# Seven block products for eight in four K-tile pairs of the down product

## The chip, the cores and the metric

The kernel is one program on one core of a Trainium2 chip. The time is the device time of one execution in microseconds (us); the result of a comparison is the ratio of the times of two kernels that run on the same chip. A core has a matrix engine (TensorE, PE in the profile), a vector engine (VectorE, DVE), an engine for functions and copies (ScalarE, ACT), a general one (GpSimd, POOL), and a queue engine that here only starts loads (SyncE, SP). Each engine executes its own list of instructions in order and waits for others by semaphores. SP, ACT and POOL also start DMAs, which run beside the engines.

## What is computed

The kernel is one layer of a diffusion backbone on 256 latent tokens of width 2048, with 256 context tokens ahead of them. A gated linear attention and a differential attention share one input projection, are merged by gates, projected, and added to x. Then comes a gated MLP with a depthwise convolution of width 3:

```
h2 = modulate(rms_norm(x_new, norm2_w), sh2, sc2)
u = h2 @ w_up                                   # 2048 -> 2 x 5632
u = sum(pad(u)[:, j:j + T] * conv_w[j] for j in range(3)) + conv_b
gate, val = split(u, 2)
x_new = x_new + g2 * ((silu(gate) * val) @ w_down)   # 5632 -> 2048
```

Only the last line matters here: a product of the 256 x 5632 matrix g = silu(gate) * val with w_down (5632 x 2048), then the multiplication by the row g2 and the addition of x_new. All is float32. So that PE can work at its fast rate, each operand is split into a high half (rounded to the fast format, fp32r) and a low half (the rest), and a product of two blocks is three matmuls: high by high, low by high, high by low.

## The kernel before

The down product goes over two halves h of the 2048 output columns, 1024 each. Within a half it goes over 44 K tiles k of 128 rows of w_down. For a K tile, fetch (L225) starts one load of 128 x 1024 on SP into one of 4 places called raw; pieces (L1292) cuts it into two pieces of 512 columns, and split (L201) makes of each its high half whi (a cast on ACT, L206) and its low half wlo (a subtraction on DVE, L213). The halves lie in 4 places each (tags hi and lo), so that a new piece can be cast when the piece four before it has been read for the last time. For each piece, part (L1297) does three matmuls for each of the two blocks t of 128 tokens: 12 matmuls of 512 columns per K tile. They accumulate in four banks of PSUM (2 blocks of tokens by 2 blocks of columns). `after(i, chain[0])` ties each matmul of the stage behind the one before it, so PE's order is that of the program. The first half's banks are the four aux banks, the second half's the four acc banks.

g comes as 44 tiles gs[k] of 128 x 2 x 256: index 1 holds the high half, index 0 the low half. The last one is finished while the down product begins.

The residual must be added in the layout of the result (tokens on partitions), but x_new lies transposed in the C tiles (tags c0 to c15). turn(m) (L1265) transposes four of them by 4 STREAM_TRANSPOSE on DVE into one place of araw and then copies 32 pieces from there into the row tiles by 32 small DMAs that POOL starts. It is done four times. gate_line(h) (L1253) makes the row g2 for one half: a memset on POOL of a place of araw, four small DMAs on POOL that gather the values in one partition, and three that spread it to others; a STREAM_SHUFFLE on DVE (L1284) then spreads it to all partitions, into cb, and frees the place. The tag araw has two places. They were used by the loads of w_ada (with their dot products on DVE, L338) until the end of the up stage; then by two lines and four turns. done (L1307) finishes a bank: times cb, plus the row tile, both on DVE, and a store that ACT starts. residual(h, k) (L1277) puts these steps into the program behind chosen K tiles.

The order in which an engine meets its instructions is that of a planner at build time (`schedule_with_timeline_sim=True`, L1344). It goes through the program with estimates of its own of how long each instruction takes. When an engine is free in that reckoning, the planner gives it the earliest instruction of the program that is ready by then, that is, whose operands are there and whose tile has a place. So a step written far down in the program can be hoisted far up; and a step may stand far down in an engine's list because the planner reckoned that its place or its operand would come late. The list is fixed then: the chip's engines take it in that order, however long the things before truly take.

Of the kernel before, what the change touches and what calls it, by code (L numbers as in the profile page):

```python
# [9 lines left out]
F32 = mybir.dt.float32  # L10
F32R = mybir.dt.float32r
# [3 lines left out]
ALU = mybir.AluOpType  # L15
# [3 lines left out]
P = 128  # L19
D = 2048  # L20
T = 256
# [7 lines left out]
FT = FF // P  # L29
# [9 lines left out]
SWW = 32 + C0 + (NGK + 1) * P  # L39
UPS = 6  # L40
CONVS = 7
SLOTS = 12
EARLY_ADA = 4, 14
GATE_ADA = [0.25] * 4 + [0.5] * 16 + [1] * 12
# [102 lines left out]
def layer_kernel(tc, I, out):  # L147
    nc = tc.nc
    V, S, G, PE = nc.vector, nc.scalar, nc.gpsimd, nc.tensor
    es = ExitStack()  # L150
    with es:
        cp = es.enter_context(tc.tile_pool(name="const", bufs=1))
        st = es.enter_context(tc.tile_pool(name="stream", bufs=1))
        hp = es.enter_context(tc.tile_pool(name="acts", bufs=1))
        ps = es.enter_context(tc.tile_pool(name="psum", bufs=1, space=PSUM))

        def acc_bank(name):
            return ps.tile([P, 512], F32, tag="acc", bufs=4, name=name)

        def aux_bank(name, j=0):  # L160
            return ps.tile([P, 512], F32, tag=f"aux{j}", bufs=2, name=name)
# [31 lines left out]
        chain = []  # L193
# [36 lines left out]
        def split_act(hi, lo, x):  # L230
            S.copy(hi, x)
            V.tensor_tensor(lo, x, hi.bitcast(F32), op=ALU.subtract)
# [965 lines left out]
        with tc.tile_pool(name="ffn", bufs=1) as pf:  # L1198
            gs = []
            ada_buffers(st, 2)  # L1200
            temps = [0]

            def temp():

                temps[0] += 1
                return C[temps[0] % (KT - UPS)][:, 1, :]


            def conv(b, ct):
                u = temp()  # L1210
                S.activation(u, b, AF.Identity, bias=vcol("conv_b", ct), scale=vcol("conv_w", 2 * FT + ct))
                V.scalar_tensor_tensor(u[:, 1:], b[:, :T - 1], vcol("conv_w", ct), u[:, 1:],
                                       op0=ALU.mult, op1=ALU.add)
                V.scalar_tensor_tensor(u[:, :T - 1], b[:, 1:], vcol("conv_w", 4 * FT + ct), u[:, :T - 1],
                                       op0=ALU.mult, op1=ALU.add)
                return u

            def gated(j, bg, bv):
                ug = conv(bg, j)
                uv = conv(bv, FT + j)  # L1220
                after(S.activation(ug, ug, AF.Silu), silu)
                V.tensor_tensor(ug, ug, uv, op=ALU.mult)
                g = pf.tile([P, 2, T], F32R, name=f"g{j}")
                split_act(g[:, 1, :], g[:, 0, :], ug)
                gs.append(g)

            def orders(n, nq, first, last):


                shifted = [i for j in range(0, nq * (last - first + 1) - 3, 7) for i in (first * nq + j, first * nq + j + 4)]  # L1230
                q = range(n * nq, (n + 1) * nq)
                return [ENDED if i == (last + 1) * nq - 1 else SHIFTED if i in shifted else TURN for i in q]

            for j in range(UPS // 2):
# [12 lines left out]
            ada_done(48)  # L1247

            splits[1] = 0
            gt = pf.tile([P, 32], F32, name="gt")  # L1250
            rows = []

            def gate_line(h):  # L1253

                line = st.tile([P, 1024], F32, tag="araw", bufs=2, name="line")
                G.memset(line, 0.0)
                to = line[0:1, :].rearrange("o (c p j) -> o c p j", c=8, p=4)
                for p in range(4):
                    o = 32 * p + 16 + 8 * h
                    nc.gpsimd.dma_start(to[:, :, p, :], gt[o:o + 8, :])  # L1260
                for r in range(32, P, 32):
                    nc.gpsimd.dma_start(line[r:r + 1, :], line[0:1, :])
                return line

            def turn(m):  # L1265

                rows.append([hp.tile([P, 512], F32, tag=f"a{4 * t + m}", name="row") for t in range(2)])
                turned = st.tile([P, 1024], F32, tag="araw", bufs=2, name="turned").rearrange("p (c t) -> p c t", c=4)
                for c in range(4):
                    V.transpose(turned[:, c, :], x1[4 * m + c])  # L1270
                for p in range(4):
                    for q in range(8):
                        to = rows[m][q // 4].rearrange("p (c n) -> p c n", c=4)
                        nc.gpsimd.dma_start(to[32 * (q % 4):32 * (q % 4 + 1), :, 32 * p:32 * (p + 1)],  # L1274
                                            turned[32 * p:32 * (p + 1), :, 32 * q:32 * (q + 1)])

            def residual(h, k):  # L1277

                if (h, k) == (0, 2):
                    V.transpose(gt, adav[:, 32:64])  # L1280
                elif (h, k) in ((0, 3), (0, 4)):
                    lines.append(gate_line(k - 3))
                elif (h, k) in ((0, 14), (0, 15)):
                    V.stream_shuffle(cb[:, 1024 * (k - 14):1024 * (k - 13)], lines[k - 14], [0] * 32)  # L1284
                elif (h, k) in ((0, 16), (0, 17), (1, 2), (1, 3)):
                    turn(len(rows))
                elif h and 8 <= k < 12:
                    done(0, k % 2, k // 2 % 2)

            lines = []  # L1290

            def pieces(k):  # L1292

                raw = fetch(I["w_down"][h, k], 1024)
                return [split(raw[:, n * 512:(n + 1) * 512], 512) for n in range(2)]

            def part(t, n, k, w):  # L1297
                ts = slice(t * P, (t + 1) * P)
                g = gs[k]
                for a, b in ((1, 0), (0, 0), (1, 1)):  # L1300
                    i = PE.matmul(banks[h][t][n], g[:, a, ts], w[n][b], start=k == 0 and (a, b) == (1, 0),  # L1301
                                  stop=k == FT - 1 and b == 1)
                    if chain:
                        after(i, chain[0])
                    chain[:] = [i]

            def done(h, t, n, cols=slice(0, 512)):  # L1307

                o = slice(1024 * h + 512 * n + cols.start, 1024 * h + 512 * n + cols.stop)
                y = hp.tile([P, 512], F32, tag=f"a{8 + (4 * h + 2 * t + n + (cols.start > 0)) % 8}", name="y")[:, :cols.stop - cols.start]  # L1310
                V.tensor_tensor(y, banks[h][t][n][:, cols], cb[:, o], op=ALU.mult)
                V.tensor_tensor(y, y, rows[2 * h + n][t][:, cols], op=ALU.add)
                nc.scalar.dma_start(out[t * P:(t + 1) * P, o], y)

            banks = []
            for h in range(2):
                banks.append([[acc_bank("down") if h else aux_bank("down", t) for n in range(2)] for t in range(2)])
                last = FT - 2 if h else FT
                for k in range(last):
                    w = pieces(k)  # L1320
                    for n in range(2):
                        for t in range(2):
                            part(t, n, k, w)
                    residual(h, k)

            ws = [pieces(k) for k in range(last, FT)]
            for n in range(2):
                for t in range(2):
                    for k in range(last, FT):
                        part(t, n, k, ws[k - last])  # L1330
                    for cols in [slice(0, 512)] if not (n and t) else [slice(0, 256), slice(256, 512)]:
                        done(1, t, n, cols)

# [14 lines left out]
```

## Time and profile before

| | us |
|---|---|
| median of 3 runs | 1696.35 (1695.54 to 1697.02) |
| the profiled execution | 1695.98 |
| its span, first to last instruction | 1693.8 |
| PE busy | 1674.0 (99%) |
| DVE busy | 1273.2 (75%) |
| ACT busy | 980.3 (58%) |
| POOL busy | 331.4 (20%) |
| down product, first to last matmul's start | 1449.4 to 1688.6 |

Times in rows are microseconds from the span's start. A row of a timeline gives the start, the length, the engine, the line of the kernel, the operation, the tiles written and read, and in brackets the idle time before it with what ended it. PEld is the loading of PE's stationary operand, which runs beside the matmuls. A matmul's length in the records is longer than the distance to the next, since matmuls overlap. "DMA to landing" is the time from a load's issue to its arrival.

### The profile page before, as it was taken

The page shows a single profiled execution, that of the slowest core. Times are in us where ns is not written, and L with a number is a line of the kernel's source. Part 1 is how long each engine was busy: PE and PEld are TensorE (multiplying, and loading weights), DVE is VectorE, ACT ScalarE, POOL GpSimd, SP SyncE. Part 2 cuts the span into 40 slices and gives each one's busy share as a digit, 9 for nine tenths or more (in the row PEclk, how much of TensorE's full clock was granted, in tenths as well). Part 3 has the DMA queues.
Part 4 walks back from the last instruction along what each step waited for, and adds up shares of the span by engine and source line. Part 5 has one row for each costly group of instructions (what it writes and reads, how often), then busy time and mean ns, then how long its engine had stood idle before and what let it go on. Part 6 is the DMA issues. An engine that isn't in the chain of part 4 may idle for free.

```text
span 1693.8 us, 28588 instructions
## 1 busy us (share of the span) xinstructions
PE 1674.0 (99%) x10108; PEld 1444.6 (85%) x10108; DVE 1273.2 (75%) x2426; ACT 980.3 (58%) x1984; POOL 331.4 (20%) x431
## 2 busy tenths in 40 slices
PE   7999999999999999999999999999999999999998
PEld 6779899998787888888888998888888888888887
DVE  5556766767688888788998797878888787755655
ACT  5324554756355777656665686666666666544443
POOL 0000213131210100001323200222222222684000
PEclk9999999999999999999999999999999999999999
DMA  9995533434567555687877556767777676676664
GB/s 384 402 408 194 169 120 98 137 113 145 191 199 234 169 187 185 205 284 268 269 263 264 185 195 218 231 229 234 236 237 238 225 238 221 201 225 203 219 193 143
DMA packets 110830, 370.82 MB, mean 219 GB/s; under 512 B 14432, under 2 KB 19552, under 8 KB 110688
## 3 DMA queue, kind: packets, MB, share of 16 engines
q1 hardware_dynamic: 102112, 362.51, 63.9%
q10 hardware_dynamic: 4032, 4.37, 0.8%
q0 software_dynamic: 4544, 2.14, 0.6%
q8 instruction: 79, 1.29, 0.3%
q14 instruction: 63, 0.52, 0.1%
HBM read 364.73 MB, written 2.10 MB: 217 GB/s over the span
## 4 chain that ended last, share of the span: by engine, by line
PE 92%; DVE 4%; DMA 2%; ACT 1%; issue 1%; ACTq 0%; DVEq 0%
PE down L1301 14%; PE upg L262 9%; PE upv L262 9%; PE gate L262 7%; PE sweep L350 5%; PE upv L264 5%; PE upg L264 5%; PE gate L264 4%; PE mix L262 4%; PE ab L350 2%; PE mix L264 2%; PE pgb L262 2%; PE pga L262 2%; PE dk L313 2%; PE dk L315 2%; PE dk L314 2%
## 5 line engine op out<-in xcount | busy, mean ns | idle before, releaser
L206 ACT CAST whi<-wraw 128x512 fp32r<-128x512 f32 (+2 forms) x1004 | 607.2, 608 | 392.0 <-DVE wlo L213 112.0
L213 DVE TENSOR_TENSOR wlo<-wraw,whi 128x512 fp32r<-128x512 f32 (+2 forms) x932 | 637.6, 692 | 230.2 <-ACT whi L206 219.6
L262 PE MATMUL upg<-a,whi 128*128 128x512 f32 x656 | 229.0, 391 | 0.0
L262 PE MATMUL upv<-a,whi 128*128 128x512 f32 x656 | 229.0, 391 | 0.0
L1301 PE MATMUL down<-whi,g 128*128 128x512 f32 x704 | 216.9, 389 | 0.0
L264 PE MATMUL upv<-a,wlo 128*128 128x256 f32 x656 | 182.8, 280 | 0.0
L264 PE MATMUL upg<-a,wlo 128*128 128x256 f32 x656 | 182.6, 280 | 0.0
L262 PE MATMUL gate<-a,whi 128*128 128x512 f32 x512 | 180.5, 398 | 0.7 <-ACT whi L206 0.7
L213 POOL TENSOR_TENSOR wlo<-wraw,whi 128x512 fp32r<-128x512 f32 x72 | 100.5, 1395 | 387.9 <-ACT whi L206 375.3
L338 DVE CUSTOM_DVE_ANT_0 araw<-araw,cb 128x1024 f32<-128x1024 f32 x128 | 158.8, 1242 | 11.1 <-DMA araw<-in_w_ada 11.0
L1301 PEld LDWEIGHTS down<-whi,g 128*128 128x128 f32 x704 | 132.1, 188 | 27.4
L262 PEld LDWEIGHTS upv<-a,whi 128*128 128x128 f32 x656 | 122.4, 187 | 26.6
L262 PEld LDWEIGHTS upg<-a,whi 128*128 128x128 f32 x656 | 122.4, 187 | 26.5
L264 PE MATMUL gate<-a,wlo 128*128 128x256 f32 x512 | 140.4, 284 | 0.0
L1301 PE MATMUL down<-wlo,g 128*128 128x512 f32 x352 | 136.9, 389 | 0.0
L264 PEld LDWEIGHTS upv<-a,wlo 128*128 128x128 f32 x656 | 123.9, 189 | 0.5
L264 PEld LDWEIGHTS upg<-a,wlo 128*128 128x128 f32 x656 | 123.9, 189 | 0.5
L262 PEld LDWEIGHTS gate<-a,whi 128*128 128x128 f32 x512 | 94.4, 188 | 20.5 <-ACT whi L206 1.0
L264 PEld LDWEIGHTS gate<-a,wlo 128*128 128x128 f32 x512 | 96.5, 189 | 6.2 <-issue 1.8
L262 PE MATMUL mix<-a,whi 128*128 128x512 f32 x256 | 88.8, 396 | 0.0
L1301 PEld LDWEIGHTS down<-wlo,g 128*128 128x128 f32 x352 | 66.1, 188 | 13.8
L1274 POOL DMA_DIRECT2D row<-turned x128 | 69.4, 551 | 28.9 <-DVE turned L1270 19.4
(351 smaller groups left out, 3405.1 us busy)
## 6 DMA issues: line engine op xcount, KB each, us to landing
wraw<-in_w_up SPq DMA_DIRECT2D x164, 512.0 KB, 4.3
araw<-in_w_ada SPq DMA_DIRECT2D x128, 512.0 KB, 5.0
wraw<-in_w_down SPq DMA_DIRECT2D x88, 512.0 KB, 4.2
ada<-in_w_ad SPq DMA_DIRECT2D x64, 512.0 KB, 10.0
wraw<-in_w_gate SPq DMA_DIRECT2D x64, 512.0 KB, 4.4
wraw<-in_w_in SPq DMA_DIRECT2D x58, 512.0 KB, 4.1
wraw<-in_w_proj SPq DMA_DIRECT2D x32, 512.0 KB, 4.7
wraw<-in_w_out SPq DMA_DIRECT2D x32, 512.0 KB, 4.5
```

The lines of the kernel that those rows point to most:

```text
L206: copied[0] = S.copy(hi[:, :n], raw)
L213: i = e.tensor_tensor(lo[:, :n], raw, hi[:, :n].bitcast(F32), op=ALU.subtract)
L262: i = PE.matmul(b.rearrange("p (a b) -> p a b", a=2), whi[:, sl], acts[k], start=first, stop=last)
L264: i = PE.matmul(b[:, T:], wlo[:, sl], acts[k][:, 1, :], start=False, stop=last)
L313: PE.matmul(o, whi[:, sl], hi[k], start=first and j == 0, stop=False)
L314: PE.matmul(o, whi[:, sl], lo[k], start=False, stop=False)
L315: i = PE.matmul(o, wlo[:, sl], hi[k], start=False, stop=last and j == 1)
L338: i = V.tensor_tensor_reduce(raw, raw, cb[:, q * 1024:(q + 1) * 1024], 1.0, 0.0, op0=ALU.mult, op1=ALU.add, accum_out=ada2[:, j, q:q + 1])
L350: return kept(PE.matmul(*args, **kw))
L1274: nc.gpsimd.dma_start(to[32 * (q % 4):32 * (q % 4 + 1), :, 32 * p:32 * (p + 1)], turned[32 * p:32 * (p + 1), :, 32 * q:32 * (q + 1)])
L1301: i = PE.matmul(banks[h][t][n], g[:, a, ts], w[n][b], start=k == 0 and (a, b) == (1, 0), stop=k == FT - 1 and b == 1)
```

## The change

In the second half (h = 1) the K tiles 10 and 11, 18 and 19, 26 and 27, 34 and 35 are taken in pairs. For a pair, the 256 tokens by 256 rows of g and the 256 rows by 1024 columns of w_down are 2 x 2 matrices of blocks, and their product is made by Strassen's scheme (in Winograd's form) from 7 products of blocks, not 8.

- left(k) makes four sums of blocks of g on DVE and splits them, into tiles with tags a8 to a15 that were used by the up stage. It is written behind K tiles 28, 31, 34 and 37 of the first half.
- right(k), five K tiles ahead of the pair, loads the pair's two K tiles of w_down into the two places of araw (b1, b2), makes four sums t1 to t4 on DVE (tags c8 to c11), and splits them into tiles of their own (thalf, tags c0 to c7).
- seven(k) splits the blocks b11, b21 and b22 in the old way (tags hi and lo) and does the seven products: b11, b21, b22, t1, t3, t2, t4. Three go to banks of the half itself, as the other K tiles' do; the other four go to four more banks, "others" (p1, p5, p6, p7). These are the aux banks that the first half leaves when done(0, ...) has read them.
- add_others, behind the last pair, combines the four banks into four tiles on DVE; prepared multiplies these by cb and adds the rows ahead of time, so that done of the second half adds one tile as before.
- The finishing steps move. Before, the lines were written behind K tiles 3 and 4 of the first half, their shuffles behind 14 and 15, the turns behind 16 and 17 and behind 2 and 3 of the second half, and done of the first half behind 8 to 11 of the second. Now the turns are written behind 1, 2, 24 and 25 of the first half, the lines behind 36 and 37, the shuffles behind 0 and 1 of the second half, and done behind 2 to 5. The tiles y move from tags a8 to a15 to tags c8 to c11.

```diff
+PAIRS = [10, 18, 26, 34]
...
+            def left(k):
+                i = PAIRS.index(k)
+                g, h = [gs[q].bitcast(F32) for q in (k, k + 1)]
+                x, y = [hp.tile([P, 512], F32, tag=f"c{12 + j}", name="x").rearrange("p (s a t) -> p s a t", s=2, a=2)
+                        for j in range(2)]
+                one, two = slice(0, P), slice(P, T)
+                V.tensor_tensor(x[:, 0], g[:, :, two], h[:, :, two], op=ALU.add)
+                V.tensor_tensor(x[:, 1], x[:, 0], g[:, :, one], op=ALU.subtract)
+                V.tensor_tensor(y[:, 0], g[:, :, one], g[:, :, two], op=ALU.subtract)
+                V.tensor_tensor(y[:, 1], h[:, :, one], x[:, 1], op=ALU.subtract)
+                hi, lo = [hp.tile([P, 4, P], F32R, tag=f"a{8 + 2 * i + j}", name=n) for j, n in enumerate(("shi", "slo"))]
+                for j, z in enumerate((x, y)):
+                    V.tensor_tensor(z[:, :, 0, :], z[:, :, 0, :], z[:, :, 1, :], op=ALU.add)
+                    split_act(hi[:, 2 * j:2 * j + 2], lo[:, 2 * j:2 * j + 2], z[:, :, 0, :])
+                return hi, lo
+            def right(k):
+                b1, b2 = [st.tile([P, 1024], F32, tag="araw", bufs=2, name="bs") for _ in range(2)]
+                for q, b in ((k, b1), (k + 1, b2)):
+                    nc.sync.dma_start(b, I["w_down"][h, q])
+                t = []
+                for j, (x, y) in enumerate(((b1[:, 512:], b1[:, :512]), (b2[:, 512:], 0), (b2[:, 512:], b1[:, 512:]), (b2[:, :512], 1))):
+                    t.append(hp.tile([P, 512], F32, tag=f"c{8 + j}", name=f"t{j + 1}"))
+                    V.tensor_tensor(t[j], x, t[y] if isinstance(y, int) else y, op=ALU.subtract)
+                halves = []
+                for j in range(4):
+                    halves.append([hp.tile([P, 512], F32R, tag=f"c{4 * u + j}", name="thalf") for u in range(2)])
+                    split_act(*halves[j], t[j])
+                return b1[:, :512], b2[:, :512], b2[:, 512:], halves
+            def product(b, a, w, first, last):
+                for x, y in ((0, 0), (1, 0), (0, 1)):
+                    i = PE.matmul(b, a[x], w[y], start=first and (x, y) == (0, 0), stop=last and y == 1)
                     if chain:
                         after(i, chain[0])
                     chain[:] = [i]
+            def seven(k, ws):
+                first, last = k == PAIRS[0], k == PAIRS[-1]
+                b11, b21, b22, t = ws
+                S_ = [[q[:, j, :] for q in lefts[k]] for j in range(4)]
+                own, (p1, p5), (p6, p7) = banks[h], *others
+                for b, a, w in ((p1, whole(0, k), b11), (own[0][0], whole(0, k + 1), b21), (own[0][1], S_[3], b22),
+                                (p5, S_[0], t[0]), (p7, S_[2], t[2]), (p6, S_[1], t[1]), (own[1][0], whole(1, k + 1), t[3])):
+                    mine = b in (p1, p5, p6, p7)
+                    product(b, a, w if isinstance(w, list) else split(w, 512), mine and first, mine and last)
+            def four(k, ws):
+                for n in range(2):
+                    for t in range(2):
+                        product(banks[h][t][n], whole(t, k), ws[n], k == 0, k == FT - 1)
...
+            def add_others():
+                (p1, p5), (p6, p7) = others
+                c11, c12, c21, c22 = [hp.tile([P, 512], F32, tag=f"c{12 + j}", name="add") for j in range(4)]
+                both = hp.tile([P, 512], F32, tag="c8", name="both")
+                S.copy(c11, p1)
+                V.tensor_tensor(both, p6, c11, op=ALU.add)
...
+            def prepared(t, n):
+                r = adds[t][n]
+                V.tensor_tensor(r, r, cb[:, columns(1, n)], op=ALU.mult)
+                V.tensor_tensor(r, r, rows[2 + n][t], op=ALU.add)
...
-                y = hp.tile([P, 512], F32, tag=f"a{8 + (4 * h + 2 * t + n + (cols.start > 0)) % 8}", name="y")[:, :cols.stop - cols.start]
+                y = hp.tile([P, 512], F32, tag=f"c{8 + (2 * t + n + (cols.start > 0)) % 4}", name="y")[:, :cols.stop - cols.start]
                 V.tensor_tensor(y, banks[h][t][n][:, cols], cb[:, o], op=ALU.mult)
-                V.tensor_tensor(y, y, rows[2 * h + n][t][:, cols], op=ALU.add)
+                V.tensor_tensor(y, y, (adds[t][n] if h else rows[n][t])[:, cols], op=ALU.add)
...
+            def between(k):
+                if h == 0 and k in (1, 2, 24, 25):
+                    turn(len(rows))
+                if h == 0 and k == 3:
+                    V.transpose(gt, adav[:, 32:64])
+                if h == 0 and k in (36, 37):
+                    lines.append(gate_line(k - 36))
+                if h == 1 and k in (0, 1):
+                    V.stream_shuffle(cb[:, 1024 * k:1024 * (k + 1)], lines[k], [0] * 32)
+                if h == 1 and 2 <= k < 6:
+                    done(0, k // 2 - 1, k % 2)
+                if h == 0 and k in (28, 31, 34, 37):
+                    lefts[PAIRS[k // 3 - 9]] = left(PAIRS[k // 3 - 9])
+                if h and k + 5 in PAIRS:
+                    rights[k + 5] = right(k + 5)
+                if h and k == PAIRS[-1] + 2:
+                    add_others()
+                if h and 0 <= k - PAIRS[-1] - 3 < 4:
+                    prepared(*divmod(k - PAIRS[-1] - 3, 2))
...
+                if h:
+                    others = [[aux_bank("others", t) for n in range(2)] for t in range(2)]
                 last = FT - 2 if h else FT
                 for k in range(last):
+                    if h and k in PAIRS:
+                        seven(k, rights.pop(k))
+                    elif not (h and k - 1 in PAIRS):
+                        four(k, pieces(k))
+                    between(k)
```

More of the change, by code (lines that the diff above doesn't have):

```diff
@@ L1275, in turn @@
                                             turned[32 * p:32 * (p + 1), :, 32 * q:32 * (q + 1)])
[L1277 to L1288, printed above, removed]
@@ L1290, in layer_kernel @@
-            lines = []
+            def left(k):
[13 more added lines that the diff above has]
+                return hi, lo
@@ new lines, in product, with whole @@
+            def product(b, a, w, first, last):
+                for x, y in ((0, 0), (1, 0), (0, 1)):
+                    i = PE.matmul(b, a[x], w[y], start=first and (x, y) == (0, 0), stop=last and y == 1)
+                    if chain:
+                        after(i, chain[0])
+                    chain[:] = [i]
+            def whole(t, k):
+                return [gs[k][:, a, t * P:(t + 1) * P] for a in (1, 0)]
+            def seven(k, ws):
[7 more added lines that the diff above has]
+                    product(b, a, w if isinstance(w, list) else split(w, 512), mine and first, mine and last)
@@ L1295, in pieces @@
                 return [split(raw[:, n * 512:(n + 1) * 512], 512) for n in range(2)]
[L1297 to L1305, printed above, removed]
+            def add_others():
[4 more added lines that the diff above has]
+                V.tensor_tensor(both, p6, c11, op=ALU.add)
+                V.tensor_tensor(c12, p5, both, op=ALU.add)
+                V.tensor_tensor(c21, p7, both, op=ALU.add)
+                V.tensor_tensor(c22, p5, c21, op=ALU.add)
+                adds.extend([[c11, c12], [c21, c22]])
@@ L1307, in done, with columns @@
+            def columns(h, n, cols=slice(0, 512)):
+                return slice(1024 * h + 512 * n + cols.start, 1024 * h + 512 * n + cols.stop)
+            def prepared(t, n):
+                r = adds[t][n]
+                V.tensor_tensor(r, r, cb[:, columns(1, n)], op=ALU.mult)
+                V.tensor_tensor(r, r, rows[2 + n][t], op=ALU.add)
             def done(h, t, n, cols=slice(0, 512)):
-                o = slice(1024 * h + 512 * n + cols.start, 1024 * h + 512 * n + cols.stop)
-                y = hp.tile([P, 512], F32, tag=f"a{8 + (4 * h + 2 * t + n + (cols.start > 0)) % 8}", name="y")[:, :cols.stop - cols.start]
+                o = columns(h, n, cols)
+                y = hp.tile([P, 512], F32, tag=f"c{8 + (2 * t + n + (cols.start > 0)) % 4}", name="y")[:, :cols.stop - cols.start]
@@ L1311, in done @@
                 V.tensor_tensor(y, banks[h][t][n][:, cols], cb[:, o], op=ALU.mult)
-                V.tensor_tensor(y, y, rows[2 * h + n][t][:, cols], op=ALU.add)
+                V.tensor_tensor(y, y, (adds[t][n] if h else rows[n][t])[:, cols], op=ALU.add)
                 nc.scalar.dma_start(out[t * P:(t + 1) * P, o], y)
-            banks = []
+            def between(k):
[17 more added lines that the diff above has]
+                    prepared(*divmod(k - PAIRS[-1] - 3, 2))
@@ L1316, in layer_kernel @@
+            lines, banks, adds, lefts, rights = [], [], [], {}, {}
             for h in range(2):
                 banks.append([[acc_bank("down") if h else aux_bank("down", t) for n in range(2)] for t in range(2)])
+                if h:
+                    others = [[aux_bank("others", t) for n in range(2)] for t in range(2)]
                 last = FT - 2 if h else FT
                 for k in range(last):
[L1320 to L1323, printed above, removed]
@@ L1324, in layer_kernel @@
-                    residual(h, k)
+                    if h and k in PAIRS:
[3 more added lines that the diff above has]
+                    between(k)
             ws = [pieces(k) for k in range(last, FT)]
@@ L1329, in layer_kernel @@
                     for k in range(last, FT):
-                        part(t, n, k, ws[k - last])
+                        product(banks[1][t][n], whole(t, k), ws[k - last][n], False, k == FT - 1)
                     for cols in [slice(0, 512)] if not (n and t) else [slice(0, 256), slice(256, 512)]:
```

## The prediction, written before the result was known

> **What bounds the kernel now.** I read the page first, then the two halves of the down product as two windows, then the rows of its matmuls, and after that the timelines of the engines that feed it.
>
> ```profile
> span 1693.8 us, 28588 instructions
> PE 1674.0 (99%) x10108; PEld 1444.6 (85%) x10108; DVE 1273.2 (75%) x2426; ACT 980.3 (58%) x1984; POOL 331.4 (20%) x431
> ...
> 1449.40:1569.30 119.90, 119.90 (x531) 99.28 (x530) 71.76 (x119) 56.52 (x93) 76.67 (x142) 1.00 0.71 212
> 1569.30:1689.00 119.70, 119.67 (x528) 98.74 (x527) 66.19 (x98) 52.83 (x85) 0.00 (x0) 1.00 0.59 187
> ...
> L1301 PE MATMUL down<-whi,g x704: 387/389/397, 1449.4 to 1688.4; 128*128 128x512 f32 x176
> L1301 PE MATMUL down<-wlo,g x352: 388/389/398, 1449.9 to 1688.6; 128*128 128x512 f32 x176
> ```
>
> The windows' columns are length, then busy time of PE, weight loads, DVE, ACT and POOL, the granted clock, the DMA share and GB/s. PE has no idle time in the first half (119.90 of 119.90) and next to none in the second, while DVE is busy for 66.19 of 119.70 there. The stage is 704 + 352 = 1056 matmuls whose first starts at 1449.4 and whose last starts at 1688.6: (1688.6 - 1449.4) / 1055 = 0.2267 us from one to the next. A K tile of one half is 12 of them, 2.72 us, and its two pieces of weights 1.36 us each. So matmuls taken away here shorten the kernel, as long as everything that they wait for is there in time.
>
> How far ahead the pieces are made shows in a steady stretch:
>
> ```profile
> 1600.41 0.62 PE L1301 MATMUL down<-whi,g 128*128 128x512 f32 x2
> ...
> 1601.09 0.62 PE L1301 MATMUL down<-whi,g 128*128 128x512 f32 x2
> ...
> 1601.74 0.62 ACT L206 CAST whi<-wraw 128x512 fp32r<-128x512 f32 x1 [0.74 <-DVE wlo L213]
> ...
> 1602.39 0.69 DVE L213 TENSOR_TENSOR wlo<-wraw,whi 128x512 fp32r<-128x512 f32 x1 [0.67 <-ACT whi L206]
> ```
>
> The piece that PE starts at 1600.41 is read as whi for the last time until 1601.09 + 0.62 = 1601.71, and at 1601.74 the cast into its place begins. That is for the piece four later (four places), which PE starts at 1600.41 + 4 x 1.36 = 1605.85. Its wlo ends at 1603.08: pieces are ready about 2.8 us before use, and DVE may be late by that much without PE noticing.
>
> **The change part by part.** What is removed: in each of 4 pairs of K tiles 8 products of three matmuls become 7, so 12 matmuls go: 12 x 0.2267 = 2.72 us. Nothing else on PE changes in number or shape.
>
> What is added to DVE and ACT is much more, so its cover counts. The sums of the left side need a row for 128x256, and the eight steps that finish the first half show how DVE's extra work has been borne so far:
>
> ```profile
> L231 ACT CAST g<-C 128x256 fp32r<-128x256 f32 x1 | 0.4, 407 | 0.3 <-DVE C L1222 0.3
> ...
> 1442.56 0.42 DVE L1222 TENSOR_TENSOR C<-C,C 128x256 f32<-128x256 f32 x1
> ...
> 1567.64 1.28 DVE L1311 TENSOR_TENSOR y<-down,cb 128x512 f32<-128x512 f32 x2
> 1568.84 0.68 DVE L213 TENSOR_TENSOR wlo<-wraw,whi 128x512 fp32r<-128x512 f32 x1
> 1569.44 0.68 DVE L1312 TENSOR_TENSOR y<-y,row 128x512 f32<-128x512 f32 x1
> 1570.05 0.68 DVE L1311 TENSOR_TENSOR y<-down,cb 128x512 f32<-128x512 f32 x1
> ...
> 1571.85 0.68 DVE L213 TENSOR_TENSOR wlo<-wraw,whi 128x512 fp32r<-128x512 f32 x1
> ```
>
> left() is six operations of 0.42 and two of half that width (between 0 and 0.42, say 0.3), 3.1 us, four times 12.5. right() is four subtractions and four low halves of 0.69, 5.5 us, four times 22; b11, b21 and b22 save one low half per pair (-2.8), add_others and prepared bring twelve operations of 0.69 (8.3). Together 40 us on DVE, which is idle for 48.1 us of the first window and 53.5 of the second; ACT gets 8 casts of 0.4, 12 more of 0.62 and a copy, some 11 us, and is idle for over 60 in each. I cost all this at nothing: the idle time of both hides it. Operations start 0.60 apart in the rows (1569.44, 1570.05), so if the eight operations of a right() came in one block, DVE would be away for 4.8 us, 2.0 over the 2.8; without that cover it costs 4 x 2.0 = 8.0 us. The eight steps of done() above were such a load, held one low half back by about 2 us (3.01 between 1568.84 and 1571.85, where 1.36 is the pace), and PE did not stop. A wait for y to leave before c8 is written again at the very end I cost at nothing too: four stores lie between.
>
> **What is moved decides.** In before, the planner gives the two places of araw to the gate lines first, then to the four turns; now all turns come first and the lines last, and the first right() needs the places that the lines leave. These are the rows of DVE and POOL for this work:
>
> ```profile
> 1445.00 2.31 DVE L338 CUSTOM_DVE_ANT_0 araw<-araw,cb 128x1024 f32<-128x1024 f32 x1
> ...
> 1449.68 0.20 DVE L1280 STREAM_TRANSPOSE gt<-adav 128x32 f32<-128x32 f32 x1
> ...
> 1455.57 0.69 DVE L213 TENSOR_TENSOR wlo<-wraw,whi 128x512 fp32r<-128x512 f32 x1 [0.18 <-ACT whi L206]
> ...
> 1461.57 1.32 DVE L1284 STREAM_SHUFFLE cb<-line 128x1024 f32<-128x1024 f32 x1
> ...
> 1463.38 1.42 DVE L1270 STREAM_TRANSPOSE turned<-C 128x256 f32<-128x256 f32 x4
> ...
> 1465.30 1.31 DVE L1284 STREAM_SHUFFLE cb<-line 128x1024 f32<-128x1024 f32 x1
> ...
> 1467.70 1.41 DVE L1270 STREAM_TRANSPOSE turned<-C 128x256 f32<-128x256 f32 x4
> ...
> 1501.00 1.42 DVE L1270 STREAM_TRANSPOSE turned<-C 128x256 f32<-128x256 f32 x4
> ...
> 1536.37 1.42 DVE L1270 STREAM_TRANSPOSE turned<-C 128x256 f32<-128x256 f32 x4
> ...
> 1465.46 9.25 POOL L1274 DMA_DIRECT2D row<-turned  x17 [5.72 <-DVE wlo L213]
> 1475.73 25.64 POOL L1274 DMA_DIRECT2D row<-turned  x47 [1.01 <-DMA row<-turned]
> 1502.71 17.32 POOL L1274 DMA_DIRECT2D row<-turned  x32 [1.34 <-DVE turned L1270]
> 1538.07 7.59 POOL L1274 DMA_DIRECT2D row<-turned  x14 [18.04 <-DVE turned L1270]
> ```
>
> A turn takes POOL 17.3 us (the row of 32). Yet the third and fourth transpose stand 1536.37 - 1501.00 = 35.4 us apart, and POOL sat idle for 18.04 us before the fourth. Nothing on the chip held DVE back there; its order did. An engine executes its instructions in the order that the planner wrote, and the planner puts a hoisted one where, by its own estimate, its place comes free. So it reckons 35 us for a turn's 32 copies, twice the true time. The written positions are not the limit: the third turn stands behind the second half's K tile 2 and came some 19 K tiles into the first.
>
> Now the new order by that reckoning. The first turn can begin at about 1452 (the last dots leave araw at 1447.3, DVE first waits again before 1455.57; by bounds 1447 to 1455). Four turns of 35.4 and the transposes end POOL's work at 1452 + 1.4 + 141.6 = 1595. A line then takes what it took from gt to its shuffle, 1461.57 - 1449.68 = 11.9 us: the planner has the first shuffle at about 1607 and the second 3.7 us (1465.30 - 1461.57) or more later. But PE reaches the first pair, K tile 10 of the second half, at 1449.4 + 54 x 2.72 = 1596.3. The planner sees PE stop there and leaves DVE nothing in between, so on the chip, too, the shuffles stand on DVE behind the last low half of K tile 9: 1594.9 - 2.8 = 1592.1. POOL has the lines by 1560 or so; DVE comes to them late. From there the chain goes:
>
> ```profile
> L227 SPq DMA_DIRECT2D wraw<-in_w_down x87: 327/328/328, 1440.5 to 1673.8; - x87
> ...
> DMA to landing us min/median/max: 3.2/4.2/6.2
> ```
>
> First shuffle 1.3 us, to 1593.4. Eight steps of done(), which the planner has ready at once and which free the four banks of the other sums, 8 x 0.60 = 4.8, to 1598.2. Second shuffle 1.3, to 1599.5; it frees the place of b2. Load of b2, 4.2, to 1603.7. Subtractions t2, t3, t4, 1.8, to 1605.5; their low halves and those of b21 and b22, 5 x 0.60 = 3.0, to 1608.5. The last of b22's matmuls and the four products behind it, 13 x 0.2267 = 2.9: 1611.4. The pair should have ended at 1596.3 + 21 x 0.2267 = 1601.1. PE stands still for 10.3 us. Every matmul of the stage is tied behind the one before it, so all that follow wait; the fetches on SP are four K tiles ahead and do not matter, and later pairs find araw free 16 us (six K tiles) before they need it.
>
> Bounds: if the second shuffle goes ahead of four of the steps (-2.4), the load takes 3.2 (-1.0) and b21's and b22's halves go before the others (-2.3), 4.6 us; if the load takes 6.2 (+2.0) and two pieces of K tile 12 slip in (+1.2), 13.5 us. I take 10.4, the order of the program, since that is what ranks ready instructions. The sum: -2.72 + 10.4 = +7.7. The profiled execution is 1695.98 (span 1693.8 and 2.2 around it), so 1703.7; the median of the runs is 0.37 higher, so 1704.0, with 1698.2 to 1707.1 as this case's own range.
>
> **A pause and the clock.** The same shapes early in this run:
>
> ```profile
> 6.49 3.76 PE L350 MATMUL sweep<-ident,ccol_s 128*128 128x128 f32 x16 [6.49 <-DMA ident<-in_ident]
> ...
> 25.29 1.05 PE L350 MATMUL sweep<-ident,ccol_s 128*128 128x128 f32 x8
> ```
>
> After 6.49 us without work 16 matmuls took 3.76 us, in full run 8 take 1.05: the pause cost 3.76 - 2.10 = 1.7 us. The chain above leaves PE without work from about 1600 (p1 done) to the landing of b2, over 4 us, so the same 1.7 may be paid again behind it. [...]
>
> **The rivals.**
> Lines in time (faster, within what can be told): if the planner puts the lines early enough for DVE to reach the second shuffle before about 1588 on its way, all is ready at 1596.3 and only the 12 matmuls count: 1696.35 - 2.72 = 1693.6. For it: POOL truly needs only 17.3 us per turn, and the positions written in the program fit that pace. Against it: 35.4 us between transposes. It decides from 0.9 us per copy in the planner's reckoning instead of 1.1 (35.4 / 32).
> Blocks on DVE: the lines are in time, but each right() comes as one block; at half of the 8.0 us above 1693.6 + 4.0 = 1697.6. Against it: the done() rows.
> Forecast plus cold clock: 1704.0 + 1.7 = 1705.7.
> The pace isn't PE's: a cast and a low half one after the other take 0.62 + 0.69 and a little, also 1.36. If that set the pace, the missing matmuls would gain nothing: 1696.35. Against it: the spacing of the matmuls is the same while DVE lags and catches up around 1570.
>
> **How the numbers follow.** Forecast 0.42, with the cold clock 0.18, lines in time 0.24, blocks 0.11, no effect 0.05. About 0.2% (3.4 us) is what a measurement of this kernel can tell from no change: faster is below 1692.96, slower above 1699.74. The forecast's low end gives 0.04 to no change and the blocks' high end 0.04 to slower; with the cold clock that makes slower 0.42 + 0.18 - 0.04 + 0.04 = 0.60. Lines in time lies 0.6 us short of faster, which I give 0.03. The rest, 0.37, is the same. Both signs hold much, so the range runs from the second case to the top of the third: 1693.2 to 1708.0.
>
> **What would show it.** In the profile after: transposes of turns some 35 us apart from about 1452 on; both shuffles only near 1592 to 1600, behind the low halves of K tile 9; loads of b1 and b2 issued right behind them; one idle stretch of PE of 5 to 13 us at about 1597, and none at the pairs 18, 26 and 34; 1044 matmuls 0.2267 apart elsewhere. I am wrong if the shuffles stand before about 1588, if PE has no gap in the down product, or if the gaps come at every pair.

## The result and the profile after

The changed kernel takes 1704.4 us (median of 6 runs, 1703.79 to 1706.35) where the kernel before took 1695.7 beside it: the ratio is 1.0054, with a 95% interval of 1.0043 to 1.0065. It is slower by half a per cent. The forecast was 1704.0. The profiled execution took 1703.79, 7.8 more than that of before.

The page of the changed kernel, and the rows of its matmuls in the down product:

```profile
PE 1675.6 (98%) x10096; PEld 1443.2 (85%) x10096; DVE 1305.1 (77%) x2498; ACT 988.2 (58%) x2005; POOL 330.5 (19%) x431
...
L1320 PE MATMUL down<-whi,g x648: 387/389/796, 1448.4 to 1696.1; 128*128 128x512 f32 x162
L1320 PE MATMUL down<-wlo,g x324: 388/389/793, 1448.9 to 1696.3; 128*128 128x512 f32 x162
```

PE has 12 matmuls fewer (10096 for 10108), as it should, and yet the stage goes from 1448.4 to 1696.3, 247.9 us where it was 239.2. DVE has 32 us more work. Three windows of the stage (length, then busy time of PE, weight loads, DVE, ACT, POOL, then the granted clock) show where PE lost time:

```profile
1449.00:1595.90 146.90, 146.56 (x647) 121.02 (x646) 93.48 (x167) 68.95 (x117) 78.41 (x144) 1.00 0.70 210
1595.90:1611.17 15.27, 8.78 (x22) 4.78 (x20) 12.71 (x22) 6.58 (x12) 0.00 (x0) 0.66 0.64 213
1611.17:1691.00 79.83, 79.83 (x352) 66.08 (x353) 58.22 (x92) 41.24 (x69) 0.00 (x0) 1.00 0.54 168
```

All but a little of it lies between 1595.90 and 1611.17, the first pair of K tiles. The other three pairs lie in the last window, without a gap. The timelines of PE and DVE there:

```profile
1595.90 0.39 PE L1320 MATMUL down<-wlo,g 128*128 128x512 f32 x1
1598.29 1.13 PE L1320 MATMUL others<-whi,g 128*128 128x512 f32 x2 [2.00 <-ACT whi L207]
1600.01 0.79 PE L1320 MATMUL others<-wlo,g 128*128 128x512 f32 x1 [0.59 <-DVE wlo L214]
1604.55 1.22 PE L1320 MATMUL down<-whi,g 128*128 128x512 f32 x2 [3.74 <-ACT whi L207]
...
1611.51 0.64 PE L1320 MATMUL down<-whi,g 128*128 128x512 f32 x2
...
1591.32 0.69 DVE L214 TENSOR_TENSOR wlo<-wraw,whi 128x512 fp32r<-128x512 f32 x1 [0.67 <-ACT whi L207]
...
1591.93 1.30 DVE L1386 STREAM_SHUFFLE cb<-line 128x1024 f32<-128x1024 f32 x1
1593.27 2.48 DVE L1373 TENSOR_TENSOR y<-down,cb 128x512 f32<-128x512 f32 x4
1595.67 2.49 DVE L1374 TENSOR_TENSOR y<-y,row 128x512 f32<-128x512 f32 x4
...
1598.09 1.29 DVE L1386 STREAM_SHUFFLE cb<-line 128x1024 f32<-128x1024 f32 x1
...
1603.80 0.69 DVE L1310 TENSOR_TENSOR t<-bs,t 128x512 f32<-128x512 f32 x1 [1.87 <-DMA bs<-in_w_down]
```

Read it from the bottom: the first sum that needs b2 starts at 1603.80, when the load lands. The load could go out only when the second shuffle had freed its place, at 1599.4. That shuffle stood on DVE behind the eight steps that finish the first half, and these behind the first shuffle at 1591.93, which follows the last low half of K tile 9. POOL had the lines ready long before:

```profile
1520.20 9.60 POOL L1275 DMA_DIRECT2D row<-turned  x17 [15.31 <-DVE turned L1271]
...
1550.41 1.43 POOL L1263 DMA_DIRECT2D line<-line  x3 [1.58 <-DMA line<-gt]
```

The last copy of the second line starts by 1552, some 40 us before DVE comes to it. POOL also waited 15.31 us for the fourth turn's transposes, as in the kernel before.

### The profile page after: what moved, and what is told of

It is laid out like the page before. It is cut to its first block, busy times and chain, and to the rows that moved or that the text cites. A ratio compares the mean times of both kernels' runs of the same rounds, so it can differ in the third digit from the quotient of the medians.

```text
span 1701.5 us, 28668 instructions
## 1 busy us (share of the span) xinstructions
PE 1675.6 (98%) x10096; PEld 1443.2 (85%) x10096; DVE 1305.1 (77%) x2498; ACT 988.2 (58%) x2005; POOL 330.5 (19%) x431
## 4 chain that ended last, share of the span: by engine, by line
PE 89%; DVE 6%; ACT 2%; DMA 2%; issue 1%; DVEq 0%; ACTq 0%
PE down L1320 10%; PE upg L263 9%; PE upv L263 9%; PE gate L263 7%; PE sweep L351 5%; PE upv L265 5%; PE upg L265 5%; PE gate L265 4%; PE mix L263 4%; DVE wlo L214 2%; PE ab L351 2%; PE mix L265 2%; PE pgb L263 2%; PE pga L263 2%; PE dk L314 2%; PE dk L316 2%
## 5 line engine op out<-in xcount | busy, mean ns | idle before, releaser
L207 ACT CAST whi<-wraw 128x512 fp32r<-128x512 f32 (+2 forms) x988 | 596.7, 608 | 366.2 <-PE upg L263 77.2
L214 DVE TENSOR_TENSOR wlo<-wraw,whi 128x512 fp32r<-128x512 f32 (+2 forms) x916 | 624.7, 691 | 193.8 <-ACT whi L207 183.3
L1320 PE MATMUL down<-whi,g 128*128 128x512 f32 x648 | 200.2, 390 | 3.7 <-ACT whi L207 3.7
L1320 PEld LDWEIGHTS down<-whi,g 128*128 128x128 f32 x648 | 121.7, 188 | 29.3 <-ACT whi L207 4.3
L1320 PE MATMUL down<-wlo,g 128*128 128x512 f32 x324 | 126.7, 391 | 0.3 <-DVE wlo L214 0.3
L1320 PEld LDWEIGHTS down<-wlo,g 128*128 128x128 f32 x324 | 60.9, 188 | 14.4 <-DVE wlo L214 1.8
```

The costliest lines, as they stand in the source:

```text
L207: copied[0] = S.copy(hi[:, :n], raw)
L214: i = e.tensor_tensor(lo[:, :n], raw, hi[:, :n].bitcast(F32), op=ALU.subtract)
L1320: i = PE.matmul(b, a[x], w[y], start=first and (x, y) == (0, 0), stop=last and y == 1)
```

## The experiments

The theory is that the sums of Strassen's scheme cost PE nothing and that the first pair waits for the gate lines, whose shuffles the planner put late on DVE because it reckons a small copy on POOL at twice its true time. The rivals: the sums or the products have a price of their own (blocks on DVE), the moved steps cost by themselves, or it is their written order and not the reckoned time.

**Places of their own for b1 and b2**, in the order of the changed kernel:

```diff
-                b1, b2 = [st.tile([P, 1024], F32, tag="araw", bufs=2, name="bs") for _ in range(2)]
+                b1, b2 = [[hp.tile([P, 512], F32, tag=f"c{c + n}", name="bs") for n in range(2)] for c in (14, 12)]
                 for q, b in ((k, b1), (k + 1, b2)):
-                    nc.sync.dma_start(b, I["w_down"][h, q])
+                    for n in range(2):
+                        nc.sync.dma_start(b[n], I["w_down"][h, q, :, n * 512:(n + 1) * 512])
...
```

> As the changed kernel, but b1 and b2 are loaded into places that no line holds (tags c12 to c15). Late-lines theory: the loads and sums of the first pair are done ahead of time, but the first shuffle and done(0, ...) keep their place on DVE (planner's reckoning), now behind the low halves that PE's stop allows, so the first product waits for its bank only: a gap of 1 to 4 us at the first pair instead of 10.3, no half clock behind it, and a time 6 to 9 us under the changed kernel's: 1695.5 to 1698.5. Rival (blocks of sums on DVE or the seven products themselves are what costs): the gap stays above 6 us, 1701 or more.

Measured: 1707.15 us, ratio 1.0071 (1.0057 to 1.0085). Slower still: the theory missed the time, and by the numbers alone (1701 or more, a gap above 6 us) the rival would be right. The PE and DVE timelines tell which it was:

```profile
1601.46 0.70 PE L1321 MATMUL others<-whi,g 128*128 128x512 f32 x2 [3.23 <-DVE y L1374]
...
1609.20 0.80 PE L1321 MATMUL others<-thalf,shi 128*128 128x512 f32 x1 [5.43 <-ACT thalf L232]
...
1599.31 1.28 DVE L1387 STREAM_SHUFFLE cb<-line 128x1024 f32<-128x1024 f32 x1
...
1604.23 1.28 DVE L1387 STREAM_SHUFFLE cb<-line 128x1024 f32<-128x1024 f32 x1
...
1607.82 0.68 DVE L1311 TENSOR_TENSOR t<-bs 128x512 f32<-128x512 f32 x1
```

The halves of b11, b21 and b22 now come in time, so DVE gets to the first shuffle later (1599.31 for 1591.93), and the first product waits 3.23 us for its bank, as expected. What I had left out is a second place that is shared: t1 to t4 lie in c8 to c11, and the tiles y of done(0, ...) have these first. So the sums still stood behind the shuffles, at 1607.82, and PE waited for them another 5.43 us. The half pace that the expectation ruled out came too: behind that second stop a matmul takes 0.63 us and the next starts 0.42 later (1613.26 and 1613.68), where ahead of it matmuls took 0.39 and came 0.23 apart (1603.15 and 1603.38). The wait moved from one shared place to another; the late lines behind it are the same.

**The lines first**: the lines, their shuffles and the first two turns are written where the kernel before has them; b1 and b2 stay in araw.

```diff
-                if h == 0 and k in (1, 2, 24, 25):
+                if h == 0 and k in (16, 17, 24, 25):
                     turn(len(rows))
-                if h == 0 and k == 3:
+                if h == 0 and k == 2:
                     V.transpose(gt, adav[:, 32:64])
-                if h == 0 and k in (36, 37):
-                    lines.append(gate_line(k - 36))
-                if h == 1 and k in (0, 1):
-                    V.stream_shuffle(cb[:, 1024 * k:1024 * (k + 1)], lines[k], [0] * 32)
+                if h == 0 and k in (3, 4):
+                    lines.append(gate_line(k - 3))
+                if h == 0 and k in (14, 15):
+                    V.stream_shuffle(cb[:, 1024 * (k - 14):1024 * (k - 13)], lines[k - 14], [0] * 32)
```

> As the changed kernel, but the gate lines, their shuffles and the first two turns are written where the kernel before has them; b1 and b2 still use araw. Late-lines theory: the shuffles stand near 1465 and done(0, ...) at 1567 to 1575, the banks are free in time, b1 gets its place from the third turn at about 1571 by the planner's reckoning; b2 waits for the fourth turn's copies, which the planner ends at about 1607, so its load goes out behind PE's stop in the planner's list, on the chip at about 1592: a gap of 2 to 6 us, time 1696 to 1700. Rival (the place does not matter, only the bank): no gap, 1693.

Measured: 1697.8 us, ratio 1.0012 (1.0003 to 1.0021), within the theory's 1696 to 1700. PE, DVE and the load queue of this kernel at the first pair:

```profile
1598.13 0.73 PE L1320 MATMUL down<-whi,g 128*128 128x512 f32 x2 [1.36 <-ACT whi L207]
...
1605.10 0.63 PE L1320 MATMUL down<-whi,g 128*128 128x512 f32 x2
...
1597.38 0.69 DVE L1310 TENSOR_TENSOR t<-bs,t 128x512 f32<-128x512 f32 x1 [4.21 <-DMA bs<-in_w_down]
...
1592.47 8.37 SPq L1306 DMA_DIRECT2D bs<-in_w_down  x3
```

The load of b2 goes out at 1592.47, where 1592 was expected, DVE waits 4.21 us for it, and K tile 12, due 4.76 us after the pair's start at 1595.93, begins at 1605.10, 4.4 us late. Its place was free on the chip soon after 1557.5, when POOL ended the fourth turn's copies; that the load stands so late in SP's list fits a planner that reckons with them until about 1607, as expected.

**Both edits together.**

> Both edits: b1 and b2 in places of their own and the lines first. Late-lines theory: nothing of the first pair is late, no gap of PE in the down product, only the 12 matmuls count: 0.9984 of the kernel before, 1693.0 (1692.5 to 1694.5). Rival (the sums on DVE or the products have a price of their own): gaps at one or all pairs and a time at or above the kernel before.

Measured: 1692.76 us, ratio 0.9983 (0.9974 to 0.9992). This is the 12 matmuls and nothing else (expected 0.9984). Matmul rows, shuffles and windows of this kernel:

```profile
L1321 PE MATMUL down<-whi,g x648: 387/389/397, 1449.1 to 1685.3; 128*128 128x512 f32 x162
L1321 PE MATMUL down<-wlo,g x324: 388/389/397, 1449.6 to 1685.5; 128*128 128x512 f32 x162
...
L1387 DVE STREAM_SHUFFLE cb<-line x2: 1315/1316/1317, 1461.3 to 1465.0; 128x1024 f32<-128x1024 f32 x2
...
1449.00:1570.00 121.00, 121.00 (x536) 100.18 (x535) 82.65 (x154) 59.66 (x101) 76.75 (x142) 1.00 0.71 221
1570.00:1685.00 115.00, 115.00 (x509) 95.24 (x508) 85.50 (x135) 58.90 (x97) 0.00 (x0) 1.00 0.55 182
```

PE is busy for all of both windows, all four pairs in them. The stage lasts 1685.5 - 1449.1 = 236.4 us, 2.8 under that of before. DVE has 31 us more work than before (1304.6 for 1273.2) and costs PE nothing. That settles the rival of a price of their own, for this order of the work.

**Half of the copies on SP**, in the written order and the places of the changed kernel:

```diff
-                        nc.gpsimd.dma_start(to[32 * (q % 4):32 * (q % 4 + 1), :, 32 * p:32 * (p + 1)],
+                        (nc.sync if p % 2 else nc.gpsimd).dma_start(to[32 * (q % 4):32 * (q % 4 + 1), :, 32 * p:32 * (p + 1)],
```

> As the changed kernel in its written order and its places, but half of the turns' small copies (odd p) are started by SP and not by POOL. Late-lines theory: POOL's work in the planner's reckoning falls from 142 to 71 us, so the shuffles come before 1575 and all is in time for K tile 10 of the second half: no gap there, about 1693 if SP's 64 extra issues do not hold up its fetches, up to 1695 if they do at places. Rival (the written order, lines behind turns, is what costs): the gap stays, 1704.

Measured: 1708.8 us, ratio 1.0082 (1.0068 to 1.0096). Shuffles, the window of the first pair (which PE reaches only at 1612.83 here), and the start of the stage:

```profile
L1386 DVE STREAM_SHUFFLE cb<-line x2: 1316/1316/1317, 1532.5 to 1536.6; 128x1024 f32<-128x1024 f32 x2
...
1608.00:1620.00 12.00, 12.00 (x55) 9.94 (x54) 7.70 (x13) 6.13 (x11) 0.00 (x0) 1.00 0.63 212
...
1448.54 20.86 SPq L1275 DMA_DIRECT2D row<-turned  x32
...
1474.67 1.22 PE L1320 MATMUL down<-whi,g 128*128 128x512 f32 x2 [14.22 <-ACT whi L207]
```

With POOL's reckoned work halved and the written order unchanged, the shuffles come at 1532.5 and 1536.6 (1591.93 and 1598.09 in the changed kernel) and the gap at the pair is gone. PE comes to the pair 17 us later than in the changed kernel, but the shuffles stand some 75 us ahead of it, so the gap would be gone without that delay too. So the written order alone doesn't make the lines late: it puts them behind the turns, and the reckoned time of the turns' copies says how far. The time is 13.8 us above the theory's 1695 for another reason, which I had undersized at up to 2 us: 32 copies hold SP for 20.86 us, the fetches of w_down stand behind them, and PE has nothing for 14.22 us at 1460.

**Later pairs**, K tiles 20, 25, 30 and 35 (`PAIRS = [20, 25, 30, 35]`):

> As the changed kernel, but the pairs are K tiles 20, 25, 30 and 35 of the second half instead of 10, 18, 26 and 34; the steps keep their written order and their places. Late-lines theory: PE reaches the first pair at 1449 + 64 x 2.72 = 1623, the shuffles stand at their reckoned 1605 to 1615 without any stop of PE before them, and the loads and sums follow by 1623 or little later: a gap of 0 to 2 us at the first pair, none at the others although they are closer together; with the 0.6 us that the early transposes cost at 1450, 1692.5 to 1696. Rival (the first pair pays a price of its own wherever it stands): a gap of about 10 us at 1623 and 1704.

Measured: 1696.5 us, ratio 1.0004 (0.9996 to 1.0013). The 10 us are gone, so the first pair has no price of its own; but the time lies 0.5 us above the stated range. The stage is 4.5 us longer than with both edits (1449.9 to 1690.8), with small stops of PE: 0.33 us at 1452 behind the early transposes, 0.77 at 1614 behind the shuffles and the steps of done, 0.25 at 1620, and the largest just ahead of 1664.77:

```profile
1664.77 0.50 PE L1320 MATMUL down<-wlo,g 128*128 128x512 f32 x1 [0.81 <-DVE wlo L214]
...
1660.41 0.69 DVE L1310 TENSOR_TENSOR t<-bs,t 128x512 f32<-128x512 f32 x1
1661.02 0.69 DVE L1310 TENSOR_TENSOR t<-bs 128x512 f32<-128x512 f32 x1
1661.62 0.69 DVE L233 TENSOR_TENSOR thalf<-t,thalf 128x512 fp32r<-128x512 f32 x1
1662.22 0.69 DVE L1310 TENSOR_TENSOR t<-bs,t 128x512 f32<-128x512 f32 x1
1662.82 1.29 DVE L233 TENSOR_TENSOR thalf<-t,thalf 128x512 fp32r<-128x512 f32 x2
1664.03 0.69 DVE L214 TENSOR_TENSOR wlo<-wraw,whi 128x512 fp32r<-128x512 f32 x1
```

At this last one the rival "blocks on DVE" is real: six operations of a right() in a row, 3.6 us, and the next low half is late by 0.81 us of PE's time.

**The moved order alone**, without any pair (`PAIRS = []`, the second half's done adds the rows as before):

> The moved finishing steps without any pair: turns, lines, shuffles and done(0, ...) are written where the changed kernel has them and y has its tags, all K tiles are taken by eight products. Late-lines theory: the shuffles come at about 1605 to 1615 too, but nothing waits for them before the end, so no gap but the 0.6 us at 1450: 1695.4 to 1697. Rival (the moved steps disturb DVE or the loads by themselves): a gap in the second half, 1698 or more.

Measured: 1698.12 us, ratio 1.0016 (1.0007 to 1.0024), 1.1 us above the theory's range and where the rival put it (1698 or more). DVE and PE around the shuffles:

```profile
1602.98 1.32 DVE L1386 STREAM_SHUFFLE cb<-line 128x1024 f32<-128x1024 f32 x1
...
1604.79 2.48 DVE L1373 TENSOR_TENSOR y<-down,cb 128x512 f32<-128x512 f32 x4
...
1608.39 1.31 DVE L1386 STREAM_SHUFFLE cb<-line 128x1024 f32<-128x1024 f32 x1
...
1610.19 1.90 DVE L1374 TENSOR_TENSOR y<-y,row 128x512 f32<-128x512 f32 x3
...
1612.74 0.50 PE L1320 MATMUL down<-wlo,g 128*128 128x512 f32 x1 [0.77 <-DVE wlo L214]
```

The shuffles come at 1603 and 1608, about where they were expected, and PE waits for none of them. But two shuffles and eight steps in nine microseconds leave room for three low halves (at 1604.20, 1607.18 and 1609.59), and PE stops for 0.77 us. With the transposes ahead of the first low halves at 1450 this makes the stage 2.0 us longer than before (1448.5 to 1689.7). That explains most of the 2.5 us; the rest is within the spread of the runs. So the rival is right in kind: the moved steps cost some 2 us by themselves, by crowding the low halves on DVE at two places.

**Five pairs**, K tiles 8, 14, 20, 26 and 32, on top of both edits; the fifth pair's left sums are made behind K tile 12 of the second half, in a place of araw and in the tiles of the first pair's sums.

> As the kernel with both edits (places of their own for b1 and b2, lines first), but five pairs, K tiles 8, 14, 20, 26 and 32, the sums of the fifth made in the second half. If only the number of matmuls counts, 15 x 0.2267 = 3.4 us under the kernel before: 1692.0, 0.7 under four pairs. If DVE can't bear a pair every six K tiles (5.5 us of sums and 3.1 for the fifth pair on top of 8.3 in 15.6 us), gaps at the pairs of 1 us or more and a time of 1693 to 1697.

Measured: 1692.43 us, ratio 0.9982 (0.9973 to 0.9991). The stage goes from 1449.1 to 1684.9, 235.8 us: 0.6 less than with four pairs where 0.7 was expected, and PE has no stop. The interval can't tell the two kernels apart; both beat the kernel before and the changed one.

## Why the prediction was right, and where it was off

The gain term held: 12 matmuls at 0.2267, 2.72 us, came out as 2.8 of stage time once nothing else was in the way. The cause held, and nearly every time of the chain did:

| step | forecast | measured |
|---|---|---|
| first turn's transposes start | 1452 (1447 to 1455) | 1446.89 |
| third to fourth turn's transposes on DVE | 35.4 apart | 1484.48 to 1518.48: 34.0 |
| first shuffle starts | 1592.1 | 1591.93 |
| eight steps of done end | 1598.2 | 1598.1 |
| second shuffle ends | 1599.5 | 1599.4 |
| b2 lands | 1603.7 | 1603.80 |
| pair ends | 1611.4 | 1611.5 |

The rows of the first two lines, from the changed kernel's DVE timeline:

```profile
1446.89 1.41 DVE L1271 STREAM_TRANSPOSE turned<-C 128x256 f32<-128x256 f32 x4
1448.88 1.41 DVE L1271 STREAM_TRANSPOSE turned<-C 128x256 f32<-128x256 f32 x4
...
1484.48 1.42 DVE L1271 STREAM_TRANSPOSE turned<-C 128x256 f32<-128x256 f32 x4
1518.48 1.42 DVE L1271 STREAM_TRANSPOSE turned<-C 128x256 f32<-128x256 f32 x4
```

K tile 9's last matmul starts at 1595.90, so K tile 12 was due at 1596.13 + 21 x 0.2267 = 1600.9 and came at 1611.51: 10.6 us late, where the sum took 10.4. PE did not stand still in one stretch of 10.3 us, though, as the sum and the sign had it: it stopped three times, 2.00, 0.59 and 3.74 us, and much of the rest went into matmuls at half the clock. The last part of the chain came to the right length by luck, by two errors that cancel: the planner ranked the halves of b21 and b22 ahead of those of the sums (my lower bound, -2.3), but let three low halves of the next K tiles and a sum of the next pair in between, and t4's low half came only at 1610.43. Against the kernel before beside it (1695.7) the change is 8.7 us, where the sum had 7.7; that 1704.0 and 1704.4 lie so close is luck in part, as the forecast started from 1696.35.

What the sum left out: the early transposes. It has no term for their place among DVE's first low halves. The two matmuls ahead of the one below start from 1449.96 on, so it was due two spacings later, at 1450.41, and came 0.5 us late; with the spacings around it some 0.7 were lost.

```profile
1450.92 0.51 PE L1320 MATMUL down<-wlo,g 128*128 128x512 f32 x1 [0.34 <-DVE wlo L214]
```

The work added to DVE was put too high, without harm: 40 us in the prediction, 32 in the profile (1305.1 for 1273.2). Operations in a row start 0.60 us apart, and the prediction counted each at its length of 0.69. It also took two of left()'s eight operations for half as wide; all eight are 128x256.

"I cost all this at nothing" for the sums on DVE is true for the written pairs, eight K tiles apart, and for five pairs six apart, and false as a rule: where DVE gets a block of other work, the 2.8 us of lead is used up, as the sums of the later pairs and the shuffles and steps of the moved order alone show (0.8 us a time).

The rival of the cold clock, the 1.7 us of the first pause paid once more, was half right. No run shows that the clock made the 1.7: in the kernel before, the granted clock is 1.00 from 6.49 to 10.25, over the 16 matmuls that it was read from. But at the pair the clock did fall: it was 0.50 from 1598.60 to 1606.00 and matmuls came 0.43 apart.

```profile
1598.60:1606.00 7.40, 3.06 (x6) 1.13 (x6) 4.84 (x8) 2.74 (x6) 0.00 (x0) 0.50 0.63 209
...
1606.77 0.63 PE L1320 MATMUL down<-whi,slo 128*128 128x512 f32 x1
1607.20 0.63 PE L1320 MATMUL down<-wlo,shi 128*128 128x512 f32 x1
...
1610.43 0.69 DVE L233 TENSOR_TENSOR thalf<-t,thalf 128x512 fp32r<-128x512 f32 x1
```

The 1.7 us were not paid on top, though: the pair's last matmul needed t4's low half, which DVE, busy without a pause from 1603.80, ended at 1611.1, and by then PE had caught up at half pace. Nor did the clock fall where the rival had it, in the wait for b2. It was at 0.50 behind the stop of 2.00 us, before those of 0.59 and 3.74. In the first experiment it was still at 1.00 at the end of a stop of 3.23 us, from 1598.23 to 1601.46:

```profile
1598.00:1601.40 3.40, 0.23 (x2) 0.00 (x0) 2.71 (x6) 0.62 (x1) 0.00 (x0) 1.00 0.01 2
```

Of these two stops it was the shorter behind which the clock fell.

Lines in time, the faster rival, was what the change is worth when its work is placed well: both edits gave 1692.8 where it said 1693.6. Its condition (the second shuffle before 1588) just wasn't met by the order as it was written.

## What to carry to other kernels

The 12 matmuls saved were worth their spacing, 2.8 us, only where all that they wait for came early (both edits); as written the change cost 8.7 us. So before adding up savings follow each new operand back through the places it shares: here the price was in the place of a buffer, not in any new work. In these lists an instruction's position followed what the planner reckoned, not the chip's time: with half of the copies taken from POOL and the written order unchanged, the first shuffle came at 1532.5 and not at 1591.93. So an instruction that comes late in an engine's list although its operands and its place were long there (the second line's last copy began by 1552) points to an estimate that is too long, and the distance between such instructions points to its size (here 34 to 35 us between two turns that POOL does in 17.3; the planner's own figure was not read). A shared tag that is freed only by a late step should be taken off the path for all tiles that the new work needs, since freeing one alone (b1 and b2, but not t1 to t4) moved the wait and made it longer (1707.15 us for 1704.4).

## What the runs showed of the hardware that was not expected

A small copy between tiles held SP longer than it holds POOL: 32 of them took SP 20.86 us (0.65 each), where POOL takes 0.55 for one in the changed kernel. The large fetches stood behind them in SP's list, the next at 1469.50, and PE stopped for 14.22 us. I had expected at most 2.

In these runs the length of a stop of PE did not tell what its clock does. It fell to 0.50 behind a stop of 2.00 us in the changed kernel, and stood at 1.00 through one of 3.23 us in the first experiment, where the half pace came only behind the next, of 5.43.
